# Moving the router's transposes, four low parts and two layout copies in a mixed decoder trunk

## The chip, the cores and the metric

The kernel runs on one core of one Trainium2 chip. The metric is the device time of one execution in microseconds. The kernel before takes 1474.78 us, the median of three runs (1474.64 to 1475.36). The engines are TensorE (PE: matrix products, with PEld for its weight loads), VectorE (DVE), ScalarE (ACT), GpSimd (POOL) and SyncE (SP), which hands the weight transfers to the DMA queue.

## The reference

Two decoder layers over 256 tokens of width 1024. Layer 0 mixes tokens with gated linear attention and channels with a dense SwiGLU; layer 1 mixes with softmax attention (called fox here) and channels with a mixture of 8 experts, of which each token takes 2. The part that matters is the expert layer and the norm ahead of it:

```python
h = rms_norm(x, norm_gain[i, 1]) * (1.0 + sc2) + sh2
logits = (h @ w_router).astype(jnp.float32) + b_router.astype(jnp.float32)
top_vals, top_idx = lax.top_k(logits, TOP_K)
top_w = jax.nn.softmax(top_vals, axis=-1)
combine = jnp.sum(jax.nn.one_hot(top_idx, N_EXPERTS, dtype=jnp.float32)
                  * top_w[..., None], axis=-2)
for e in range(N_EXPERTS):
    y = y + combine[..., e:e + 1].astype(h.dtype) * swiglu(h, w_gate[e], w_up[e], w_down[e])
x = x + g2 * y
```

All values are float32. One expert has three matrices of 1024 x 3584 (14.7 MB each), so the eight experts' weights are 352 MB.

## The kernel before, in words

**Staging.** Every weight comes from memory in 1 MB tiles `raw` (ring of 7, in the expert stage 10). In the attention layers and for half of the experts each tile is split into a rounded high part `whi` (ScalarE, line 224) and the rest `wlo` (VectorE or GpSimd, line 226), and a product is then three passes: high by high, high by low, low by high. The helper `split` may make a tile in several parts, may give some low parts to GpSimd, and may put its high and low parts behind named instructions.

**The router stage**, in the order of the data:

- The attention's output projection `foxo` (lines 247 to 249) ends in eight blocks of 128 columns. `Norm.update` adds each to the residual `xT` (VectorE, line 352), squares it (ScalarE, `n_sq_moe` for block 0 and `n_t_moe` for the others, lines 361 and 364; three `n_t` buffers), adds the squares of blocks 1 to 5 into `n_sq_moe` (GpSimd, line 366), and makes the scaled pair `hr_moe_h` (ScalarE, line 378) and `hr_moe_l` (VectorE, line 379). TensorE sums `n_sq_moe` and the squares of blocks 6 and 7 over the channels into `n_ss_moe` (line 372).
- `narrow` multiplies the pair by the router's weights into `rlogT` (8 blocks, two products each, lines 493 and 494), copies it to `rlog_t` (VectorE), and turns it to tokens in rows, `rlog`, with four small products (lines 503 to 506).
- `Norm.col` makes the root `n_moe_r` (GpSimd, line 423) from `n_ss_moe`.
- `residual` transposes `xT` into four banks `xr` of PSUM, 16 transposes of 128x128 (TensorE, line 992). `tokens` makes the token pair `m_h` (ScalarE, line 1030) and `m_l` (VectorE, line 1032) from it, and `residual_out` copies it to `xres`.
- `positions` makes the logits `rlg`, compares them in pairs (`req`, `rgt`), sums and thresholds to the mask `msk` (VectorE, lines 1012 to 1017), and counts places with three small products `pos`. The one-hot `oh` follows.
- `gather` (line 1137) multiplies the token pair by the one-hot: 32 passes for the first expert, which give its input `g`. The counts `cnt` (line 1047) feed `ranks`, VectorE's chain of small steps (`rkc`, `rku`, `rkm`, `rkt`) that ends in `order`, the experts sorted by load. SyncE reads `order` (line 1271) to know which expert's weights come after those of expert 0's first stage, which are already loaded.
- The expert loop then alternates a large slot (split weights) with a small one (raw weights, two column halves, line 1256).

`hows` gives the first four weight tiles of the expert stage their treatment; the second has all four low parts on GpSimd, the third two of four.

**What sets the order.** A scheduler puts the instructions of each engine into a fixed order by their dependences, by a simulated time and by priority: what is wrapped in `urgent` comes first. `after(i, ...)` adds an order against the instruction `i`, without a wait, to those instructions of the block that run on the engine of `i`; to instructions of other engines it adds nothing. Within an engine the order is then kept on the chip, and a first instruction that waits holds all behind it. `first` is a dictionary of such instructions: `r` is the root on GpSimd, `msk` the mask on VectorE, `hi` the last token copy on ScalarE, `lo` the one-hot on VectorE, `g` the last low part of `g` on VectorE.

The layout copies `g2s` (line 1111, called `gs` in the trace, since both are slices of one tile) put the expert gate's two halves one above the other for the small slots.

## Time and profile before

| | |
|---|---|
| median of three runs | 1474.78 us |
| the profiled execution's own time | 1478.52 us |
| its span | 1476.8 us |
| TensorE busy | 1419.3 us (96%) |
| VectorE busy | 961.7 us (65%) |
| ScalarE busy | 695.1 us (47%) |
| GpSimd busy | 80.5 us (5%) |
| bytes moved by the weight queue | 486.87 MB |

The span runs from the first to the last instruction of the profiled execution, whose own time is 3.7 us above the median. Starts in the trace are microseconds from the start of the span. A busy share is an average over stages; the router stage, near 570 to 606 us, is short, and its order is read from the timeline and from the chain of waits. A product appears in two passes where its operands are full float32, so that a count in the trace can be twice that of the program. In a timeline the last brackets give the idle time before an instruction and what ended it.

### The profile page before, as it was taken

How to read it: one execution, taken by the hardware profiler on the slowest of the kernel's cores; microseconds unless marked ns; L12 is line 12 of the kernel's file. 1: busy time of each engine (PE TensorE's matmuls, PEld its weight loads, DVE VectorE, ACT ScalarE, POOL GpSimd, SP SyncE). 2: the span in 40 equal slices, each digit the busy share in tenths (PEclk: the TensorE clock that was granted, in tenths of full speed). 3: DMA queues.
4: the chain of work that ended last, by engine and by line, in shares of the span. 5: the costliest groups of instructions: out<-in, count | busy, mean ns of one | idle time of the engine just before them, and what ended most of it. 6: DMA issues, size and time to landing. Idle time of an engine off the chain costs nothing.

```text
span 1476.8 us, 21633 instructions
## 1 busy us (share of the span) xinstructions
PE 1419.3 (96%) x8443; PEld 1073.4 (73%) x8443; DVE 961.7 (65%) x1292; ACT 695.1 (47%) x982; POOL 80.5 (5%) x87
## 2 busy tenths in 40 slices
PE   6999999999999998999999999999999999999996
PEld 2899999999999997864756664656475556475453
DVE  7786897778977786662744764556574456574353
ACT  3653644344565565552644463445264346254241
POOL 2000200000132124000000000000000000000000
PEclk9999999999999999899999999999999999999998
DMA  9996578898865432699999999999999999999994
GB/s 318 362 340 226 189 269 313 296 345 279 286 178 161 127 103 86 252 403 395 409 402 402 409 409 409 409 402 402 409 409 409 409 401 404 409 409 408 410 398 189
DMA packets 183000, 488.86 MB, mean 331 GB/s; under 512 B 10815, under 2 KB 51913, under 8 KB 182890
## 3 DMA queue, kind: packets, MB, share of 16 engines
q1 hardware_dynamic: 182602, 486.87, 87.7%
q8 instruction: 68, 1.11, 0.3%
q10 hardware_dynamic: 288, 0.52, 0.1%
q14 instruction: 42, 0.34, 0.1%
HBM read 486.32 MB, written 1.05 MB: 330 GB/s over the span
## 4 chain that ended last, share of the span: by engine, by line
PE 81%; DMA 9%; DVE 7%; issue 1%; SPq 1%; ACT 0%; DVEq 0%; ACTq 0%
PE mo L1256 8%; PE mo L243 6%; PE mo L241 6%; PE mo L242 6%; PE md L1256 6%; DMA raw<-in_moe_w_up_dram 4%; PE gu L247 3%; DVE wlo L226 3%; PE gu L249 3%; PE gu L248 3%; PE md L243 3%; DMA raw<-in_moe_w_down_dram 3%; PE md L242 3%; PE md L241 3%; PE dn L247 2%; PE dn L248 2%
## 5 line engine op out<-in xcount | busy, mean ns | idle before, releaser
L226 DVE TENSOR_TENSOR wlo<-raw,whi 128x1024 fp32r<-128x1024 f32 (+2 forms) x481 | 569.0, 1232 | 92.2 <-ACT whi L224 90.9
L224 ACT CAST whi<-raw 128x1024 fp32r<-128x1024 f32 (+2 forms) x491 | 487.5, 1051 | 262.4 <-PE gu L248 67.3
L1256 PE MATMUL mo<-raw,gs 128*64 128x512 f32 (+1 forms) x1024 | 203.7, 543 | 9.9 <-DMA raw<-in_moe_w_up_dram 8.4
L241 PE MATMUL mo<-whi,g 128*128 128x512 f32 x448 | 175.9, 393 | 0.0
L242 PE MATMUL mo<-whi,g 128*128 128x512 f32 x448 | 175.5, 392 | 0.0
L1256 PEld LDWEIGHTS mo<-raw,gs 128*64 128x64 f32 x1024 | 70.3, 137 | 131.1 <-issue 95.5
L243 PE MATMUL mo<-wlo,g 128*128 128x512 f32 x448 | 153.0, 399 | 1.0 <-DVE wlo L226 0.5
L1352 DVE TENSOR_TENSOR msg<-msg,mo 128x512 f32<-128x512 f32 (+1 forms) x16 | 9.9, 620 | 171.6 <-PE mo L1256 171.6
L243 PEld LDWEIGHTS mo<-wlo,g 128*128 128x128 f32 x448 | 83.2, 189 | 35.9 <-issue 13.8
L1256 PE MATMUL md<-raw,gs 128*64 128x512 f32 x448 | 108.8, 603 | 0.0
L241 PEld LDWEIGHTS mo<-whi,g 128*128 128x128 f32 x448 | 84.6, 189 | 19.2 <-issue 1.6
L242 PEld LDWEIGHTS mo<-whi,g 128*128 128x128 f32 x448 | 84.7, 189 | 18.1
L322 DVE SCALAR_TENSOR_TENSOR adacc<-raw,csil,adacc 128x1024 f32<-128x1024 f32 x70 | 90.0, 1286 | 10.3 <-DMA raw<-in_ada_w_dram 9.9
L249 PE MATMUL gu<-h_ffn_h,wlo 128*128 128x256 f32 x320 | 90.5, 284 | 0.0
L248 PE MATMUL gu<-h_ffn_l,whi 128*128 128x256 f32 x320 | 90.1, 282 | 0.0
L247 PE MATMUL gu<-h_ffn_h,whi 128*128 128x256 f32 x320 | 89.9, 283 | 0.0
L241 PE MATMUL md<-whi,act_h 128*128 128x512 f32 x192 | 76.7, 400 | 0.5 <-ACT whi L224 0.5
L242 PE MATMUL md<-whi,act_l 128*128 128x512 f32 x192 | 76.1, 397 | 0.0
L1350 ACT ACTIVATE msg<-mo 128x512 f32<-128x512 f32 (+1 forms) x16 | 8.7, 544 | 132.6 <-PE mo L1256 132.6
L1175 ACT CAST act_h<-actT 128x512 fp32r<-128x512 f32 x24 | 13.3, 589 | 116.2 <-PE actT L1240 116.2
L1256 PEld LDWEIGHTS md<-raw,gs 128*64 128x64 f32 x448 | 28.2, 136 | 51.5 <-issue 51.2
L243 PE MATMUL md<-wlo,act_h 128*128 128x512 f32 x192 | 62.2, 398 | 1.4 <-DVE wlo L226 1.3
(488 smaller groups left out, 2706.1 us busy)
## 6 DMA issues: line engine op xcount, KB each, us to landing
raw<-in_moe_w_gate_dram SPq DMA_DIRECT2D x112, 1024.0 KB, 17.1
raw<-in_moe_w_up_dram SPq DMA_DIRECT2D x112, 1024.0 KB, 16.3
raw<-in_moe_w_down_dram SPq DMA_DIRECT2D x112, 1024.0 KB, 16.9
raw<-in_ada_w_dram SPq DMA_DIRECT2D x48, 1024.0 KB, 7.1
raw<-in_fox_w_in_dram SPq DMA_DIRECT2D x16, 1024.0 KB, 5.9
raw<-in_ffn_w_gate_dram SPq DMA_DIRECT2D x14, 1024.0 KB, 5.3
raw<-in_ffn_w_up_dram SPq DMA_DIRECT2D x14, 1024.0 KB, 6.5
raw<-in_ffn_w_down_dram SPq DMA_DIRECT2D x14, 1024.0 KB, 5.3
```

The lines of the kernel that those rows point to most:

```text
L224: nc.scalar.copy(hi[:, s], raw[:, s])
L226: (nc.gpsimd if i in pool else nc.vector).tensor_tensor(lo[:, s], raw[:, s], hi[:, s].bitcast(F32), op=ALU.subtract)
L241: nc.tensor.matmul(ps, ah, wh, start=first, stop=False)
L242: nc.tensor.matmul(ps, al, wh, start=False, stop=False)
L243: return nc.tensor.matmul(ps, ah, wl, start=False, stop=last)
L247: i = nc.tensor.matmul(ps, wh, ah, start=first, stop=False)
L248: nc.tensor.matmul(ps, wh, al, start=False, stop=False)
L249: nc.tensor.matmul(ps, wl, ah, start=False, stop=last)
L322: nc.vector.scalar_tensor_tensor(a, raw[:, kk, :], csil[:, k:k + 1], a, op0=ALU.mult, op1=ALU.add)
L1175: acts["i"] = nc.scalar.copy(ah, v)
L1256: nc.tensor.matmul(ps[64 * i:64 * (i + 1), 0:n], a, w[:, i * n:(i + 1) * n], start=first, stop=last)
L1352: nc.vector.tensor_mul(sg, sg, ps[:, 0:hw])
```

## The change

Three edits. The 16 transposes of `residual` get an order behind the last router product. The second weight tile's low parts, which are GpSimd's, were named to come behind the root `first["r"]`, and are now named to come behind the mask `first["msk"]`. The two layout copies are traced after the first gather, with an order behind its last low part.

```diff
-        nc.tensor.matmul(ps[0:n, 0:c], w[:, 0:n], xl, start=False, stop=last)
+        return nc.tensor.matmul(ps[0:n, 0:c], w[:, 0:n], xl, start=False, stop=last)
+
+    narrow_last = {}
...
-            mm_side(ps, w[:, k], n, at(norm.raw, A_, k), k == 0, k == KD - 1)
+            narrow_last["i"] = mm_side(ps, w[:, k], n, at(norm.raw, A_, k), k == 0, k == KD - 1)
...
-        xps = residual()
+        with after(narrow_last["i"]):
+            xps = residual()
...
-        for i in range(2):
-            nc.vector.tensor_copy(g2s[64 * i:64 * (i + 1), :], g2[64 * i:64 * (i + 1), 512 * i:512 * (i + 1)])
...
         urgent(gather)(0, 0, oh0)
+        with after(first["g"]):
+            for i in range(2):
+                nc.vector.tensor_copy(g2s[64 * i:64 * (i + 1), :], g2[64 * i:64 * (i + 1), 512 * i:512 * (i + 1)])
...
-        hows = [(4,), (4, range(4), (), (first["r"],)), (4, range(2), (first["hi"],), (first["lo"],)),
+        hows = [(4,), (4, range(4), (), (first["msk"],)), (4, range(2), (first["hi"],), (first["lo"],)),
```

GpSimd from the end of the projection to the root, before (`wlo` 128x1024 belongs to the projection, 128x512 to the experts):

```order
L226 TENSOR_TENSOR wlo<-raw,whi 128x1024 x4
L366 TENSOR_TENSOR n_sq_moe<-n_sq_moe,n_t_moe_6408 128x256
L366 TENSOR_TENSOR n_sq_moe<-n_sq_moe,n_t_moe_6441 128x256
L366 TENSOR_TENSOR n_sq_moe<-n_sq_moe,n_t_moe_6444 128x256
L366 TENSOR_TENSOR n_sq_moe<-n_sq_moe,n_t_moe_6485 128x256
L366 TENSOR_TENSOR n_sq_moe<-n_sq_moe,n_t_moe_6488 128x256
L423 TENSOR_TENSOR n_moe_r<-n_moe_v,nhalf 128x2
L226 TENSOR_TENSOR wlo<-raw,whi 128x512 x6
```

The same place on GpSimd in the changed kernel:

```order
L226 TENSOR_TENSOR wlo<-raw,whi 128x1024 x4
L366 TENSOR_TENSOR n_sq_moe<-n_sq_moe,n_t_moe_6408 128x256
L226 TENSOR_TENSOR wlo<-raw,whi 128x512 x4
L366 TENSOR_TENSOR n_sq_moe<-n_sq_moe,n_t_moe_6441 128x256
L366 TENSOR_TENSOR n_sq_moe<-n_sq_moe,n_t_moe_6444 128x256
L366 TENSOR_TENSOR n_sq_moe<-n_sq_moe,n_t_moe_6485 128x256
L366 TENSOR_TENSOR n_sq_moe<-n_sq_moe,n_t_moe_6488 128x256
L423 TENSOR_TENSOR n_moe_r<-n_moe_v,nhalf 128x2
L226 TENSOR_TENSOR wlo<-raw,whi 128x512 x2
```

Four of the six low parts have moved from behind the root to between the first and the second addition. On ScalarE the squares of blocks 5, 6 and 7, which stood among the last scaled copies, now stand behind all of them.

TensorE from the last transposes to the small products, before (the transposes of banks 0 and 2 stand further ahead, among the projection's last products):

```order
L503 MATMUL rlog<-ident,br_c 128x8
L992 MATMUL xr_6587<-ident,xT 128x128 x2
L992 MATMUL xr_6589<-ident,xT 128x128 x4
L372 MATMUL n_ss_moe_6523<-ones,n_t_moe_6521 128x1
L372 MATMUL n_ss_moe_6524<-ones,n_t_moe_6521 128x1
L493 MATMUL rlogT<-hr_moe_h,wr 16x258
L372 MATMUL n_ss_moe_6523<-ones,n_t_moe_6529 128x1
L372 MATMUL n_ss_moe_6524<-ones,n_t_moe_6529 128x1
L494 MATMUL rlogT<-hr_moe_l,wr 8x258
```

The end of the router products on TensorE in the changed kernel:

```order
L493 MATMUL rlogT<-hr_moe_h,wr 16x258
L494 MATMUL rlogT<-hr_moe_l,wr 8x258
L994 MATMUL xr_6586<-ident,xT 128x128 x4
L994 MATMUL xr_6587<-ident,xT 128x128 x4
L994 MATMUL xr_6588<-ident,xT 128x128 x4
L994 MATMUL xr_6589<-ident,xT 128x128 x4
L505 MATMUL rlog<-ident,br_c 128x8
L506 MATMUL rlog<-two_141,rlog_t 128x8
L508 MATMUL rlog<-two_141,rlog_t 128x8 x2
```

All sixteen transposes stand behind the last `rlogT` product and ahead of all of `rlog`. The first norm sum, from `n_sq_moe`, stands directly behind the projection's last product in the changed kernel, ahead of all `rlogT` products.

VectorE at the start of the ranking, before (`rkc` is the first copy of the counts, `g` the last low part of the first gather):

```order
L1159 TENSOR_TENSOR g<-gs,g 128x256
L1048 COPY rkc<-cnt 128x8
L1049 COPY rku<-rkc 128x8
L1183 CAST ohT_6918<-oht_6915 128x256
L1050 MEMSET rku 128x1
L1159 TENSOR_TENSOR g<-gf_3_6694,g 128x256
L1052 TENSOR_TENSOR rkm<-rku 128x64
```

And in the changed kernel:

```order
L1160 TENSOR_TENSOR g<-gs,g 128x256
L1187 CAST ohT_6918<-oht_6915 128x256
L1050 COPY rkc<-cnt 128x8
L1051 COPY rku<-rkc 128x8
L1160 TENSOR_TENSOR g<-gf_3_6692,g 128x256
L1167 COPY gs<-g_145 64x512 x2
L1052 MEMSET rku 128x1
L1054 TENSOR_TENSOR rkm<-rku 128x64
```

The two layout copies now stand between the copies of the counts and the ranking's comparisons. On TensorE both transposes `oht` now stand ahead of the counts `cnt`; before, one of the two stood behind them. Three small steps of the weights (`comb`, `rsm` twice) have moved ahead of the first one-hot on VectorE.

## Rows read from the trace of the kernel before

**Rows 1.** The page: clock and traffic in 40 slices of 36.9 us.

```profile
PEclk9999999999999999899999999999999999999998
...
GB/s 318 362 340 226 189 269 313 296 345 279 286 178 161 127 103 86 252 403 395 409 402 402 409 409 409 409 402 402 409 409 409 409 401 404 409 409 408 410 398 189
```

**Rows 2.** Busy time by stretch: length, engines with counts, granted clock, transfer share, GB/s.

```profile
600.00:640.00 40.00, 40.00 (x184) 27.45 (x184) 25.53 (x49) 21.40 (x30) 0.00 (x0) 0.94 0.90 352
640.00:700.00 60.00, 60.00 (x256) 34.94 (x256) 25.20 (x24) 24.20 (x28) 0.00 (x0) 1.00 1.01 401
...
1300.00:1400.00 100.00, 96.46 (x430) 58.02 (x428) 49.91 (x47) 41.35 (x47) 0.00 (x0) 1.00 1.02 409
```

**Rows 3.** Waits of SyncE, 580 to 620 us: total, times, longest.

```profile
SPq L1271 <- DVE rku L1079: 21.4, 1, 21.4
```

**Rows 4.** SyncE's transfers in order of time: start, duration, count.

```profile
603.32 2.27 SPq L203 DMA_DIRECT2D raw<-in_moe_w_gate_dram  x4
```

**Rows 5.** Chain of waits around the router: start, length, engine, tile, line, count.

```profile
576.97 0.55 PE xr L992 x5
577.52 0.34 PE n_ss_moe L372 x4
...
578.59 0.12 PE rlogT L493
...
582.50 0.46 PE rlog L506 x4
...
583.65 0.71 DVE req L1012
584.36 1.27 DVE rgt L1013
...
588.53 0.81 DVE msk L1017
...
591.64 7.06 PE ga L1137 x32
...
598.94 0.65 PE cnt L1047 x4
599.59 0.31 PE oht L1181
...
600.71 0.43 PE mo L242
```

**Rows 6.** Busy time by stretch around the router.

```profile
580.00:584.00 4.00, 2.44 (x22) 2.02 (x20) 2.27 (x9) 1.00 (x2) 2.26 (x2) 1.00 0.37 97
584.00:585.00 1.00, 0.00 (x0) 0.00 (x0) 1.00 (x2) 1.00 (x3) 1.00 (x2) 0.61 1.02 422
592.00:600.00 8.00, 7.96 (x39) 7.69 (x38) 5.60 (x19) 4.31 (x10) 0.00 (x0) 0.50 0.01 2
604.00:605.00 1.00, 1.00 (x5) 0.79 (x4) 0.83 (x6) 0.05 (x1) 0.00 (x0) 0.65 0.73 102
```

**Rows 7.** GpSimd in order of time: start, duration, line, operation, count, idle before.

```profile
570.50 0.74 POOL L366 TENSOR_TENSOR n_sq_moe<-n_sq_moe,n_t_moe 128x256 f32<-128x256 f32 x1 [7.22 <-ACT n_t_moe L364]
573.38 3.31 POOL L366 TENSOR_TENSOR n_sq_moe<-n_sq_moe,n_t_moe 128x256 f32<-128x256 f32 x4 [2.15 <-ACT n_t_moe L364]
...
582.95 7.58 POOL L226 TENSOR_TENSOR wlo<-raw,whi 128x512 fp32r<-128x512 f32 x6
```

**Rows 8.** ScalarE in order of time, the high parts beside the norm.

```profile
570.74 2.18 ACT L224 CAST whi<-raw 128x512 fp32r<-128x512 f32 x4
```

**Rows 9.** VectorE in order of time, beside the norm and in the ranking.

```profile
574.60 2.78 DVE L379 SCALAR_TENSOR_TENSOR hr_moe_l<-xT,mod,hr_moe_h 128x256 fp32r<-128x256 f32 x4
577.30 0.86 DVE L352 SCALAR_TENSOR_TENSOR xT<-foxo,mod,xT 128x256 f32<-128x256 f32 x2
...
582.00 0.84 DVE L1111 COPY gs<-g 64x512 f32<-64x512 f32 x2
...
600.62 0.22 DVE L1052 TENSOR_TENSOR rkm<-rku 128x64 f32<-128x64 f32 x1
```

## The prediction

> **What bounds the kernel now.** I read the page's busy slices first, then the granted clock, the transfer queue, the chain of waits and last the single engines around the router. In the slices [rows 1] the traffic falls to 103 and 86 GB/s in slices 15 and 16, is 252 in the next, and then stays near 405 to the end: the experts' weights stream without a break. Over the eight stretches from 640 to 1400 us the transfer engines are full, share 1.01 to 1.03 [rows 2], so a later start of that stream is a later end, one for one. The stream starts when SyncE, which hands out the transfers, has read the list of ranked experts: it waits 21.4 us for VectorE [rows 3] and resumes at 603.32 us [rows 4]. What counts is therefore the chain up to that list [rows 5]: TensorE's norm sums (`n_ss_moe`, 577.52) and router products (`rlogT`, `rlog`, done at 582.96), VectorE's mask (583.65 to 589.34), the gathers (591.64, 7.06 us), the counts (598.94), the ranking. That is one long serial stretch, and everything the change touches lies in it or beside it.
>
> Two costs in it stand out. The gathers run with the clock at 1.2 GHz: it was full from 580 to 584, fell within 584 to 585 and was 0.50 from 592 to 600, though the gathers left TensorE no pause there [rows 6]. And VectorE's small comparisons take 1.27 us instead of about 0.3: each ends as one of GpSimd's low parts ends. GpSimd runs six of them back to back from 582.95, 7.58 us, so 1.26 each [rows 7].
>
> **GpSimd's low parts.** The edit names the mask, a VectorE instruction, as the one to queue behind. An order is kept only between instructions of one engine, and the order of the changed kernel shows that this queues nothing on GpSimd: the old edge, to GpSimd's own root `n_moe_r`, is gone, no new one came, and four parts now stand between the first and the second of the five additions into `n_sq_moe`. Their data are ready: ScalarE makes the high parts from 570.74, the first by 571.3 [rows 8], and GpSimd is free since 571.24 [rows 7]. So four parts take 571.3 to 576.35 (4 x 1.26). Three additions at 0.83 (3.31 / 4) follow, to 578.85. The last one needs its square, which ScalarE now makes behind all scaled copies. Those need the last `xT` updates of VectorE, which start at 577.30 behind four `hr_moe_l` that took 2.78 us beside GpSimd's additions [rows 9]; with GpSimd busy without a break each waits for one GpSimd instruction, and I put the updates at 578.1. Two copies and the square bring it to about 579.95, the addition to 580.7, and TensorE's first norm sum to 580.85 instead of 577.52: +3.3. (Were the square not late it would be 579.8; with the parts a tenth slower beside VectorE's work, as the additions are, 0.83 against 0.74 alone [rows 7], 581.4.) TensorE is in order, so all router products wait behind this sum, though most of their inputs are ready. Before, the same wait was not there: five transposes ran up to it.
>
> What it gives: the mask chain loses four of the six low parts that held it. From the first comparison to the mask's end it now takes 5.69 us (583.65 to 589.34). Alone, four comparisons near 0.27 (a 128x64 one takes 0.22, [rows 9]), a reduction and a threshold come to 1.55. The two parts left on GpSimd wait for high parts that ScalarE makes behind the token copies, as before, and so they fall at about the time of the comparisons: each can cost up to 1.26. Ends 1.55 and 4.1; I take 2.6, one part met in full. Gain 3.1.
>
> The Trainium skill (SBUF — State Buffer, section "Who interferes with whom") says that a VectorE instruction with two SBUF inputs contends with a GpSimd instruction that reads SBUF, and that the later one blocks for the whole of the other. By that alone the comparisons would lose four waits of 1.26 and the edit would give up to 5 us, against the 3.1 taken here; the rows [rows 5, 7] agree on the blocking, but the same rule charges the four `hr_moe_l` that the parts now run beside.
>
> **The transposes.** Sixteen of them. Before, ten stood among the projection's last products and six where TensorE waited for inputs, so they cost little. Ten leave the projection, and it ends at 576.4 instead of 576.97; that gains nothing, for the sum is not there until 580.85. All sixteen now stand between `rlogT` and `rlog`, on the path. At full clock the stretch is: 12 passes of norm sums at 0.085 (4 in 0.34), 16 products at 0.12, 16 transposes at 0.11 (5 in 0.55), 8 small `rlog` passes at 0.115 (4 in 0.46) [rows 5]: 1.02 + 1.92 + 1.76 + 0.92 = 5.62, ending at 586.5, against 582.96: +3.55. That GpSimd's reciprocal root is ready earlier than `rlog` helps nobody but the token copies.
>
> **The clock in that stretch.** TensorE now stands still from 576.4 to 580.85, 4.4 us. Before, it ran dry at 582.96 and the clock was down within 584 to 585 [rows 5, 6], at most 2 us later. So I expect it down when the norm sums begin, or soon after. Did it come back within the stretch? The gathers, of the transposes' shape, ran 7 us without raising it; the experts' dense products did, but only within 604 to 605, after some 4 us (the first still take 0.43 at 600.71) [rows 5, 6]. I take it low to the end. At that level a 512-column product takes 0.43 [rows 5], so a 258-column one 0.215; a transpose what a gather pass takes, 7.06 / 32 = 0.22; a small pass what the counts take, 0.65 / 4 = 0.163. Sum: 16 x 0.215 + 16 x 0.22 + 20 x 0.163 = 3.44 + 3.53 + 3.26 = 10.2, so `rlog` ends at 591.1, +8.15.
>
> **The two layout copies.** They leave VectorE's queue at 582.00 (0.84 us, [rows 9]), where `rlog` was not yet done: gain about 0. They now stand, with the cast `ohT`, in front of the ranking's first step on VectorE, and the counts stand behind both `oht` transposes: 0.84 of copies, of which some lies in waiting. I take +0.9 with the 0.31 of the transpose that the counts now stand behind [rows 5] (bounds 0 if all of it hides, 1.5 if none). Three small instructions of the weights have also moved ahead of the first one-hot: two behind the mask, covered by the token parts, one in front: +0.25.
>
> **Sum.** Mask: `rlog` at 591.1, comparisons 0.7 later as before, 2.6 of chain: 594.4 against 589.34, +5.1. One-hot +0.25, ranking +0.9: the stream of weights starts about 6.2 us later. Gathers low in both. The profiled execution took 1478.52 with a span of 1476.8, 3.7 above the median of the three runs, 1474.78; I add the shift to the median unchanged: 1474.78 + 6.2 = 1481.0.
>
> **Rivals.**
> - *The clock comes back during the stretch* (or falls late into it). For it: `rlogT` is dense once the sums are through. Against: the 7 us of gathers. Transposes and `rlog` at full level save 1.77 + 0.38: +4.05, 1478.8.
> - *The clock does not fall at all.* The stall is there, with full-level products: `rlog` 586.5, mask 589.8, then 0.25 and 0.9: +1.65, 1476.4; a mask chain at its upper end 1477.9. Against it: the fall after 582.96.
> - *Not slower: the gathers run at full clock.* The transposes put dense work closer to the mask, and the chain behind is shorter, 3.3 us instead of 6.4, so TensorE may enter the gathers at full level, at 0.115 instead of 0.22 a pass: 32 x 0.105 = 3.4 less, 0.1 less in the counts. It decides if the clock survives both the standstill before the sums and the one before the one-hot; on top of +1.65 it gives -1.8, 1473.0, and with both low parts missing the comparisons 1471.9. Against it: two waits, each longer than what sufficed before.
> - *The end doesn't follow the routing*, because the stream has slack that the trace hides. For it: from 600 to 640 the share is 0.90, not full. Against: share 1.01 to 1.03 from 640 on [rows 2]. About +0.7, 1475.5.
>
> **How the numbers follow.** Forecast 0.48, clock back 0.20, clock kept 0.16, gathers at full clock 0.09, no coupling 0.07. A measurement of this kernel tells about 0.2% from no change, 2.95 us, so slower is above 1477.7 and faster below 1471.8. Slower: 0.46 of the forecast, 0.16 of the second and 0.05 of the third, 0.67. Faster: half of the fourth, which with a clean mask chain stands at that bound, 0.05. The rest, 0.28, is no change. The range of 8 in 10 runs from the no-coupling case to the forecast with parts that meet the mask chain at its upper end (+1.5) and half a microsecond more in the norm: 1475.5 to 1483.0; left out are the fourth case, half of the fifth and a small tail above.
>
> **What would show it.** Right: four low parts on GpSimd between 571 and 576.5; the first norm sum near 580.9 with TensorE idle for over 4 us before it; the granted clock at half there; sixteen transposes at 0.2 each ahead of `rlog`; comparisons near 0.3 but for one or two; SyncE resuming near 609.5. Wrong: a norm sum before 579 (the parts started later or ended sooner), transposes at 0.11 (clock kept), a stream that resumes late but ends on time (slack), or gathers at 0.11.

## The result, and the profile after

The changed kernel takes 1484.62 us (median of 4 runs, 1484.45 to 1485.94), the kernel before in the same comparison 1475.07 us (4 runs, 1474.64 to 1475.80). The medians are 9.55 us apart, a ratio of 1.0065; the ratio on record is 1.0057 with a 95% interval of 1.0037 to 1.0077. So the changed kernel is slower by some 9.5 us, where 6.2 us was forecast, with 1481.0 and a range up to 1483.0. The direction is as forecast, the size is not, and the time lies outside the range.

The profiled execution of the changed kernel took 1484.45 us with a span of 1482.7 us. Between the two profiled executions the span grew by only 5.9 us (1482.7 - 1476.8). So the first thing to see is that the profiles do not hold the whole 9.5 us. Read them for what the edit did first. GpSimd of the changed kernel in order of time (start, duration, line, operation, count, idle before):

```profile
571.09 0.74 POOL L366 TENSOR_TENSOR n_sq_moe<-n_sq_moe,n_t_moe 128x256 f32<-128x256 f32 x1 [7.23 <-ACT n_t_moe L364]
572.03 5.41 POOL L226 TENSOR_TENSOR wlo<-raw,whi 128x512 fp32r<-128x512 f32 x4 [0.20 <-ACT whi L224]
577.40 2.63 POOL L366 TENSOR_TENSOR n_sq_moe<-n_sq_moe,n_t_moe 128x256 f32<-128x256 f32 x3
581.23 0.72 POOL L366 TENSOR_TENSOR n_sq_moe<-n_sq_moe,n_t_moe 128x256 f32<-128x256 f32 x1 [1.20 <-ACT n_t_moe L364]
...
591.51 2.53 POOL L226 TENSOR_TENSOR wlo<-raw,whi 128x512 fp32r<-128x512 f32 x2 [5.00 <-ACT whi L224]
```

This answers [rows 7]. The four low parts stand between the first and the second addition, as forecast, and only two parts are left for the time of the comparisons. The first addition starts 0.59 us later than before (571.09 against 570.50), which comes from ahead of the change; below, all times are counted from that addition. VectorE beside it and in the ranking, in the same columns:

```profile
574.96 4.48 DVE L379 SCALAR_TENSOR_TENSOR hr_moe_l<-xT,mod,hr_moe_h 128x256 fp32r<-128x256 f32 x4
579.37 0.86 DVE L352 SCALAR_TENSOR_TENSOR xT<-foxo,mod,xT 128x256 f32<-128x256 f32 x2
...
594.20 0.27 DVE L1016 TENSOR_TENSOR req<-req,tie 128x128 f32<-128x128 f32 x1
...
606.46 0.85 DVE L1167 COPY gs<-g 64x512 f32<-64x512 f32 x2
...
607.47 0.23 DVE L1054 TENSOR_TENSOR rkm<-rku 128x64 f32<-128x64 f32 x1
```

Against [rows 9]: four `hr_moe_l` took 4.48 us instead of 2.78 beside the low parts, and the last two `xT` updates started at 579.37 instead of 577.30. A comparison that meets no low part (594.20) takes 0.27 us. The two copies stand right ahead of the ranking's first step. The chain of waits (start, length, engine, tile, line, count), with lines that answer to [rows 5]:

```profile
582.00 1.02 PE n_ss_moe L372 x4
...
587.45 2.47 PE xr L994 x16
...
590.46 0.46 PE rlog L508 x4
...
591.61 1.32 DVE req L1014
592.93 1.27 DVE rgt L1015
...
595.15 0.17 DVE msk L1019
...
597.65 7.06 PE ga L1138 x32
...
606.16 0.76 PE mo L241
```

and the stretches of the same kernel that answer to [rows 6] (length, engines with counts, granted clock, transfer share, GB/s):

```profile
576.00:582.00 6.00, 0.99 (x9) 0.78 (x7) 5.12 (x8) 1.88 (x6) 4.59 (x6) 1.00 0.00 0
582.00:588.00 6.00, 6.00 (x32) 5.15 (x33) 0.64 (x3) 0.00 (x0) 0.71 (x1) 0.50 0.21 46
589.00:592.00 3.00, 1.90 (x17) 1.64 (x15) 0.92 (x4) 3.00 (x7) 0.49 (x1) 1.00 0.29 120
593.00:609.00 16.00, 12.45 (x51) 11.74 (x52) 12.99 (x40) 5.93 (x14) 1.04 (x1) 0.50 0.00 1
```

TensorE has 0.99 us of work from 576 to 582. From 582 to 588 the norm sums and router products run at 1.2 GHz. The clock comes back within the sixteen transposes, which take 2.47 us instead of the 3.53 that I worked out for the low level, and it is low again for the gathers, which take 7.06 us as before. SyncE's transfers in order of time, and a later stretch of the kernel:

```profile
610.16 2.31 SPq L203 DMA_DIRECT2D raw<-in_moe_w_gate_dram  x4
```

```profile
640.00:700.00 60.00, 60.00 (x254) 34.50 (x252) 30.81 (x30) 25.63 (x30) 0.00 (x0) 1.00 1.02 402
```

The stream restarts at 610.16 us instead of 603.32 [rows 3, 4], and from 640 to 700 us it is as full as before [rows 2]. From the first addition to the restart the kernel before needs 32.82 us (570.50 to 603.32) and the changed one 39.07 us: +6.25, where the prediction had +6.2. At SyncE's last write of the output the difference is 5.35 us, still counted from that addition (1469.01 for the start of the two last writes before, 1474.95 after, less 0.59): 0.9 us is given back behind the restart.

It is given back at once. ScalarE's first split of the next weights and the third group of transfers behind the restart, before and then in the changed kernel:

```profile
604.95 2.18 ACT L224 CAST whi<-raw 128x512 fp32r<-128x512 f32 x4 [4.96 <-PE mo L242]
...
617.71 11.47 SPq L203 DMA_DIRECT2D raw<-in_moe_w_down_dram  x3
```

```profile
610.41 2.19 ACT L224 CAST whi<-raw 128x512 fp32r<-128x512 f32 x4 [4.42 <-PE mo L242]
...
623.17 11.47 SPq L203 DMA_DIRECT2D raw<-in_moe_w_down_dram  x3
```

Counted from the first addition, both are 4.87 us later, not 6.25. ScalarE's split waits for TensorE's expert products. The first of these starts 5.62 us later (606.16 against 599.95, less 0.59), but the clock comes back 3.1 us behind it instead of 4.8 (granted 0.86 from 609 to 610 us here, 0.65 from 604 to 605 before [rows 6]), so that the twelfth, at which ScalarE is let go, is 4.88 later. In all fourteen profiles the third group starts 12.8 to 13.3 us behind that split, whatever the restart did. So the third group follows the expert products and no longer the moment at which SyncE reads the ranking.

So the forecast of the mechanism held in the profiles up to the restart, and some 4 us of the measured 9.5 were not in them. Executions of one and the same kernel come in groups some 4 us apart, which the mean granted clock of an execution tells apart.

| mean granted clock | runs | time, us |
|---|---|---|
| before, 0.987 to 0.990 | 48 | 1472.64 to 1477.02, median 1474.61 |
| before, 0.985 to 0.986 | 48 | 1477.57 to 1479.84, median 1479.16 |
| before, 0.980 to 0.981 | 5 | 1483.52 to 1484.20 |
| changed, 0.986 to 0.987 | 3 | 1479.80 to 1481.88 |
| changed, 0.983 to 0.984 | 9 | 1483.10 to 1485.94, median 1484.41 |

(The 101 runs of before are those of the three later comparisons; of the changed kernel the first and e5.) By their times the four runs of before in the first comparison belong to the first row; by time and clock all four of the changed kernel belong to the last; and the profile of before that the prediction was read from (1478.52 us, clock 0.986) belongs to the second row. Below, the first and the second row of before are called its short and its long form.

### The profile page after: what moved, and what is told of

Same layout as the page of the kernel before. It is cut to its first block, busy times and chain, and to the rows that moved or that the text cites. A ratio compares the mean times of both kernels' runs of the same rounds, so it can differ in the third digit from the quotient of the medians.

```text
span 1482.7 us, 21629 instructions
## 1 busy us (share of the span) xinstructions
PE 1422.3 (96%) x8443; PEld 1075.6 (73%) x8443; DVE 962.4 (65%) x1292; ACT 694.4 (47%) x982; POOL 80.2 (5%) x87
## 4 chain that ended last, share of the span: by engine, by line
PE 81%; DVE 8%; DMA 8%; issue 1%; SPq 1%; ACT 1%; POOL 0%; DVEq 0%; ACTq 0%; POOLq 0%
PE mo L1260 8%; PE mo L243 6%; PE mo L241 6%; PE md L1260 6%; PE mo L242 6%; DVE wlo L226 4%; DMA raw<-in_moe_w_up_dram 4%; PE gu L247 3%; PE gu L249 3%; PE gu L248 3%; PE md L243 3%; DMA raw<-in_moe_w_down_dram 3%; PE md L241 3%; PE md L242 3%; PE dn L247 2%; PE dn L248 2%
## 5 line engine op out<-in xcount | busy, mean ns | idle before, releaser
L1179 ACT CAST act_h<-actT 128x512 fp32r<-128x512 f32 x24 | 13.3, 589 | 115.3 <-PE actT L1244 115.3
```

The costliest lines, as they stand in the source:

```text
L1179: acts["i"] = nc.scalar.copy(ah, v)
```

## The experiments

The expectations of e1 to e4 stand under a first pair of theories: (A) in the quicker executions the gathers run at full clock, so that the router stretch itself is shorter there; (B) the difference between executions of one kernel lies outside that stretch, 570 to 606 us. e1 decided it for B. The expectations of e5 to e12 stand under the pair that followed: (A) the change costs the forecast some 6 us at the router, and the rest of the 9.5 is the distance between two forms of execution, decided long before the router; (B) the change costs 9.5 us in every form. The starts that decide between them are collected in one table, each a difference of two starts in the timelines of one kernel: from the first addition into `n_sq_moe` on GpSimd to the first norm sum, from there to the first gather, to the first expert product, and to the restart of the weight stream on SyncE (its first `raw<-in_moe_w_gate_dram`). The last two columns go on behind the restart: the start of the third group of transfers (the first `raw<-in_moe_w_down_dram`) and of the last write, each from the first addition, as a difference to before. The table counts the first norm sum of before from the timeline, where it starts at 577.36; [rows 5] has 577.52, because the chain counts its overlap with the transposes ahead of it to these.

```profile
577.36 0.51 PE L372 MATMUL n_ss_moe<-ones,n_sq_moe 128*128 128x1 f32 x4
```

| kernel | first addition at | to norm sum | to gather | to product | to restart | sum | third group | last write |
|---|---|---|---|---|---|---|---|---|
| before | 570.50 | 6.86 | 14.28 | 8.31 | 3.37 | 32.82 | 0 | 0 |
| changed | 571.09 | 10.91 | 15.65 | 8.51 | 4.00 | 39.07 | +4.87 | +5.35 |
| e1 before again | 566.20 | 6.85 | 14.30 | 8.30 | 3.37 | 32.82 | -0.14 | -0.10 |
| e2 edits 1 and 3 | 564.84 | 6.23 | 14.55 | 8.51 | 4.00 | 33.29 | +0.19 | -0.15 |
| e3 edit 2 | 570.47 | 10.53 | 13.64 | 8.52 | 3.14 | 35.83 | +3.48 | +4.41 |
| e4 low parts behind the mask | 570.92 | 6.85 | 11.10 | 10.18 | 3.44 | 31.57 | -0.79 | -0.41 |
| e5 changed again | 570.54 | 10.92 | 15.64 | 8.51 | 4.00 | 39.07 | +4.97 | +5.75 |
| e6 before, line 309 wide | 567.98 | 6.85 | 14.29 | 8.29 | 3.37 | 32.80 | -0.01 | +0.18 |
| e7 changed, line 309 wide | 566.27 | 10.92 | 15.67 | 8.51 | 4.00 | 39.10 | +4.92 | +5.75 |
| e8 edits 1 and 3, wide | 566.56 | 6.23 | 14.54 | 8.51 | 4.00 | 33.28 | -0.31 | -1.03 |
| e9 edit 2, wide | 570.81 | 10.54 | 13.68 | 8.51 | 3.13 | 35.86 | +3.42 | +4.33 |
| e10 edit 1, wide | 567.58 | 6.23 | 15.01 | 8.51 | 3.13 | 32.88 | -0.02 | +0.59 |
| e11 edit 3, wide | 567.75 | 6.85 | 14.98 | 8.30 | 4.26 | 34.39 | +0.22 | +0.29 |
| e12 as e8, low parts behind the mask | 565.08 | 6.24 | 11.75 | 10.50 | 4.21 | 32.70 | -0.34 | -0.37 |

Edit 1 is the transposes, edit 2 the low parts, edit 3 the copies. The first column moves with the form of the execution, by up to 6 us. The sum depends on the kernel alone: where a kernel ran in two forms (line 309 apart), it agrees within 0.03 us. The last column repeats less well, to 0.9 us for one and the same set of edits (e2, e8). That table separates the two things which the first comparison had mixed.

**e1: the kernel before, once more, unedited.**

> The kernel before, unchanged. Its profiled execution took 1478.5 us, its timed ones 1474.6 to 1475.8. Theory A (the routing stretch has two forms): in the quicker executions TensorE's clock is full in the gathers, which then take about 3.6 us instead of 7.1, so a profile near 1475 shows gathers of 3.6 us and a granted clock above 0.988; one near 1478.5 shows 7.1 us. Theory B (the 3.4 us of the profiled execution lie elsewhere, in the start or in the stream of weights): the gathers take 7.1 us in every profile, and what differs is the time outside 570 to 606 us.

Measured: 1474.38 us (12 runs, 1473.22 to 1479.08), ratio 0.9986 (0.9972 to 1.0001). The profiled execution took 1474.14 us, so a short form was caught. GpSimd and TensorE of it in order of time, first addition, first norm sum and first gather:

```profile
566.20 0.73 POOL L366 TENSOR_TENSOR n_sq_moe<-n_sq_moe,n_t_moe 128x256 f32<-128x256 f32 x1 [7.22 <-ACT n_t_moe L364]
```

```profile
573.05 0.51 PE L372 MATMUL n_ss_moe<-ones,n_sq_moe 128*128 128x1 f32 x4
...
587.35 0.66 PE L1137 MATMUL ga<-oh,m_h 128*128 128x128 f32 x2 [0.82 <-DVE oh L1121]
```

and one stretch far ahead of the router, of before, of the changed kernel and of this one:

```profile
138.00:144.00 6.00, 6.00 (x30) 6.00 (x30) 1.68 (x5) 0.20 (x1) 0.70 (x1) 0.51 0.04 16
```

```profile
138.00:144.00 6.00, 6.00 (x31) 6.00 (x31) 1.84 (x6) 0.59 (x4) 0.69 (x1) 0.52 0.17 64
```

```profile
138.00:144.00 6.00, 6.00 (x53) 6.00 (x53) 3.40 (x5) 2.38 (x2) 0.00 (x0) 1.00 0.00 0
```

All of the 4.3 us lies before the first addition (566.20 against 570.50). From there on the two executions agree to 0.02 us, with gathers of the same length, so A, gathers at full clock, fell, and B held. In the long form the clock is 0.51 and 0.52 from 138 to 144 us, in the short one 1.00, and TensorE is busy throughout in all three: the same stream of products, at half the clock for about 6 us. Ahead of that stretch each has two groups of one-column products of line 309 (`adat`), which start at 134.3 and 136.7 us in before and at 133.3 and 135.7 in e1.

So 1.0 us of the 4.3 is there before the fall; at the third group (208.05 against 203.75) all 4.3 are, and nearly all of the other 3 us arises in the fall. The first microsecond goes with an earlier stretch, in which the clock of before is 0.92 (its line stands under e9). In e1 it is full:

```profile
40.00:50.00 10.00, 10.00 (x84) 9.85 (x84) 8.06 (x18) 6.00 (x12) 0.57 (x2) 1.00 1.09 357
```

The seven profiles with line 309 as it was part in the same way: where the clock is 0.87 to 0.92 from 40 to 50 us (before, changed, e3, e4, e5) it falls again at 138, and where it is 1.00 there (e1, e2) it does not. So the form shows by 50 us, and the fall at 138 us follows in the late executions only.

**e2: without edit 2.**

```
-        hows = [(4,), (4, range(4), (), (first["msk"],)), ...
+        hows = [(4,), (4, range(4), (), (first["r"],)), ...
```

> The changed kernel with GpSimd's low parts back behind the root; transposes and layout copies stay moved. Theory 1 (the standstill before the first norm sum and the low clock behind it cost most): the norm sum starts near 577.5 again, the products and transposes run at full clock (0.12 and 0.11 each), rlog ends near 584.3, the mask again takes about 5.7 us beside six low parts: about 2.4 us over the kernel before in the routing stretch, some 7 less than the changed kernel. Rival (the sixteen transposes on the path cost most): it stays within 3 us of the changed kernel.

Measured: 1474.47 us (12 runs, 1472.68 to 1479.79), ratio 0.9991 (0.9975 to 1.0007). In the table edits 1 and 3 together cost 0.47 us at the restart, less than the 2.4 that was expected, and nothing at the last write: the norm sum 0.63 earlier, the product 0.47 later behind it, the restart 0.63 later behind the product. It takes edit 2 to make the kernel slower (e3).

**e3: edit 2 alone**, the same line the other way round in the kernel before.

```
-        hows = [(4,), (4, range(4), (), (first["r"],)), ...
+        hows = [(4,), (4, range(4), (), (first["msk"],)), ...
```

> The kernel before with only the edit of the low parts; transposes stand ahead of the norm sum, in its wait. Theory 1: the norm sum starts near 581.5, the clock is low behind it, rlog ends near 588.5, about 2 us sooner than in the changed kernel, the stream of weights starts about 3 us sooner (transposes 1.9, copies 0.9): 1481.5. Rival (transposes cost most): it is within 2 us of the kernel before.

Measured: 1478.96 us (12 runs, 1477.18 to 1485.39), ratio 1.0022 (1.0007 to 1.0036). TensorE in order of time:

```profile
579.28 1.16 PE L992 MATMUL xr<-ident,xT 128*128 128x128 f32 x6 [1.80 <-DVE xT L352]
581.00 0.98 PE L372 MATMUL n_ss_moe<-ones,n_sq_moe 128*128 128x1 f32 x4 [0.56 <-POOL n_sq_moe L366]
...
594.64 0.66 PE L1137 MATMUL ga<-oh,m_h 128*128 128x128 f32 x2 [0.82 <-DVE oh L1121]
```

The norm sum is late by 3.67 us, as in the changed kernel less 0.38, but six transposes are done in the wait ahead of it and none stand behind it. The stretch is 35.83 us, +3.0. So at the restart edit 2 alone costs 3.0 and edits 1 and 3 alone 0.5, but together 6.25: 2.8 us more. By the table 1.7 of these arise between norm sum and gather, where edit 1 puts sixteen transposes behind products that edit 2 has made late, and 1.0 ahead of the norm sum, where the 0.63 that edits 1 and 3 gain is lost in the wait for GpSimd and 0.38 more goes. Where the products are not late, the same transposes cost next to nothing (e10). Edits 1 and 2 without edit 3 were not run, so that the 1.7 is edit 1's alone is argued and not shown. At the last write the shares are others: edit 2 alone is 4.4 us late (the medians of e3 and e1 are 4.6 apart), edits 1 and 3 are 0.15 to 1.03 early, and the three together 5.35 to 5.75 late, 1.1 to 2.5 more than the parts.

**e4: the low parts really behind the mask.** A small addition on GpSimd reads the mask, and the six low parts are ordered behind it, so that they wait on GpSimd itself.

```
+            first["mk"] = nc.gpsimd.tensor_tensor(mk, msk[:, 0, :], msk[:, 1, :], op=ALU.add)
...
-(4, range(4), (), (first["r"],)), (4, range(2), (first["hi"],), (first["lo"],))
+(4, range(4), (), (first["mk"],)), (4, range(2), (first["hi"],), (first["lo"], first["mk"]))
```

> The kernel before with one small GpSimd addition that reads the mask, and GpSimd's six low parts ordered behind that addition, so that they really come behind the mask. Theory 1: the comparisons take about 0.3 us each, the mask's chain 1.6 us instead of 5.7; the first one-hot then meets a low part, up to 1.2 us: the stream of weights starts 2.5 to 4 us sooner, 1471 to 1472.5. With TensorE's pause 4 us shorter the gathers may also see another clock: if they run full, 3.4 us less again. Rival (the end doesn't follow the routing): no change.

Measured: 1476.68 us (12 runs, 1471.39 to 1478.49), ratio 0.9995 (0.9982 to 1.0009). The gathers start 3.2 us earlier (11.10 against 14.28 behind the norm sum), since no comparison meets a low part, but the first expert product is 1.9 later behind them: 1.25 us remains at the restart, less than the 2.5 to 4 expected, and 0.4 at the last write; the times show no gain. What the edit's words say would be worth a microsecond at the restart; the edit as it stands does something else.

**e5: the changed kernel, once more, unedited.**

> The changed kernel once more, unedited, with more runs. Theory A (executions come in two forms some 4.3 us apart, parted by the granted clock of TensorE at 137 to 144 us, long before the router; the first comparison set four executions of before in the short form against four of the changed kernel in the long one): the runs fall into two groups, near 1480 and near 1484.5, and the median ratio to before is about 1.004 (1.003 to 1.005), +6 us; a profile in the short form starts the first norm sum near 577.7 us, one in the long form near 582. Theory B (the changed kernel is 9.5 us slower in every form): all runs stand at 1483 or above and the ratio stays at 1.006 or more.

Measured: 1483.58 us (8 runs, 1479.80 to 1484.41) against 1478.81 us (31 runs), ratio 1.0039 (1.0023 to 1.0055). Three of the eight runs are at 1479.8 to 1481.9 with a clock of 0.986 or 0.987, the rest at 1483.1 to 1484.4 with 0.984: two groups, as A had it, and the difference of 9.5 us did not come again. The profile is of the long form and has the stretch of 39.07 us.

**e6: the kernel before with line 309 widened.** The edit is meant to take away what the clock fell on; e7 to e12 carry it too.

```
-                nc.tensor.matmul(ps[:, k:k + 1], a[:, k * P:(k + 1) * P], ones[:, 0:1], ...)
-            ada_out(i, j, ps[:, 0:KD])
+                nc.tensor.matmul(ps[:, 64 * k:64 * k + 64], a[:, k * P:(k + 1) * P], ones[:, 0:64], ...)
+            ada_out(i, j, ps[:, 0:64 * KD:64])
```

> The kernel before, with the 144 small products of the modulation (line 309) written with 64 equal columns instead of one; the sum reads one column of each, so what is computed is the same. Theory A: in the long form the granted clock falls from 1.00 to 0.50 at 137.5 us, behind two rows of 16 such products, and stays there until 143.5; in the short form the same products stand there and it does not fall. If these products are what the clock falls on, the fall at 137 to 144 us goes, all executions are in the short form, 1472 to 1475.5 us with no group near 1479, and the ratio to before is 0.997 to 0.999. The products themselves: between 0 and 144 x 0.1 us on TensorE, mostly beside weight loads. Rival (the form is decided by something else, earlier, at 30 to 50 us, and the fall at 137 us only follows): two groups as in before, ratio 0.9995 to 1.003. Rival (the wider products cost time of their own): one group, but at 1477 or above.

Measured: 1475.42 us (12 runs, 1474.25 to 1477.76), ratio 0.9984 (0.9974 to 0.9994). Eleven of the twelve runs lie below 1476.3, one at 1477.76, and half of them above the expected 1475.5; of the 101 runs of before 53 lie at 1477.5 or above. The stretch of 138 to 144 us:

```profile
138.00:144.00 6.00, 6.00 (x53) 6.00 (x52) 2.68 (x7) 2.58 (x3) 0.69 (x1) 1.00 0.07 25
```

The fall is gone, and with it nearly all of the long form. The earlier stretch is that of a long form, though, and the profile's first addition, at 567.98, is 1.8 us later than in e1:

```profile
40.00:50.00 10.00, 10.00 (x74) 9.85 (x74) 6.56 (x15) 5.79 (x12) 0.57 (x2) 0.88 1.09 355
```

So both hold in part, the theory and its first rival: the form shows at 30 to 50 us, and with the narrow products of line 309 the clock falls a second time in executions that were late there. With the wide ones it stays at 1.00, though their first two groups start as late as in before (134.46 against 134.34); so it does in e10 and e11, whose clock from 40 to 50 us is 0.92 and 0.91. The edit takes away the some 3 us of the fall and leaves the first microsecond. The clock also falls from 190 to 200 us, to 0.83, but there e1 has the same.

**e7: the changed kernel with line 309 widened.**

> The changed kernel with the same edit of line 309. Theory A: one group, near 1479.5 (1478.5 to 1481), so +5 to +7 us to the kernel with that edit alone and a ratio of 1.002 to 1.004 to before; granted clock 1.00 at 137 to 144 us, first norm sum near 577.5 us, and the router's stretch as in the profile of the changed kernel (TensorE idle for some 5 us, then 0.50 of the clock). Theory B (9.5 us in every form): 1482 or above.

Measured: 1480.37 us (12 runs, 1478.33 to 1484.29), ratio to before 1.0027 (1.0012 to 1.0042). TensorE and SyncE in order of time:

```profile
577.19 1.00 PE L372 MATMUL n_ss_moe<-ones,n_sq_moe 128*128 128x1 f32 x4 [5.01 <-POOL n_sq_moe L366]
```

```profile
605.37 2.32 SPq L203 DMA_DIRECT2D raw<-in_moe_w_gate_dram  x4
```

The norm sum starts at 577.19, as expected of a short form, behind the same wait of 5.01 us as in the changed kernel, and the stretch is 39.10 us. Against e6 the median is 4.95 us longer. With the long form out of the way the change costs 5 us, not 9.5. Four of the runs, at 1481.8 to 1484.3, lie above the expected group.

**e8: edits 1 and 3, line 309 widened.**

> The changed kernel without its edit 2 (GpSimd's low parts wait for the norm's column as in before) and with line 309 as in the two others: a version that may be faster than both kernels. Theory A with edits 1 and 3 worth nothing: as the kernel before with line 309 edited, within 1 us. If the copies behind the gather cost what I forecast: +0.9. If transposes behind the products bring the logits forward by what stood between the products in before (6 transposes, 0.87 us): -0.9. In numbers 1471 to 1475, ratio to before 0.996 to 0.999.

Measured: 1473.77 us (12 runs, 1472.49 to 1476.79), ratio 0.9975 (0.9962 to 0.9988), the fastest kernel here, ahead of both. Most of the gain against before is the form: the first addition stands at 566.56, without a fall at 138 us. How much of the 1.65 us between the medians of e8 and e6 belongs to edits 1 and 3 stays open: they make the stretch 0.5 us longer, as in e2, but at the last write this execution is 1.03 us ahead of before, and e2 only 0.15.

**e9: edit 2 alone, line 309 widened.**

> The kernel before with edit 2 alone and line 309 widened as in e6, so that one form of the executions is left. From the first addition of the norm on GpSimd to the restart of the weight stream on SyncE, before and e6 take 32.8 us, the changed kernel 39.1, edit 2 alone (e3) 35.8. Theory A (edit 2 costs 3.0 alone, edits 1 and 3 alone 0.5, and the remaining 2.7 come only when edit 1's sixteen transposes stand in the stretch in which the clock has fallen): 35.8 +-0.3 here, and a time of e6 + 3 = 1478.4 (1477.3 to 1479.6), ratio 1.000 to 1.002 to before, whose own runs are in two forms. Rival (e3 was a chance of its form; edit 2 costs 5 to 6 alone): 38 or more, 1480 or above.

Measured: 1480.17 us (12 runs, 1477.93 to 1483.13), ratio 1.0018 (1.0004 to 1.0033). The stretch is 35.86 us, as expected, so edit 2 alone costs 3.0 at the restart in both executions profiled, and 4.3 to 4.4 at the last write. The time missed, in part because it was added up from the 3.0: five runs lie at 1477.9 to 1478.9, the expected group, seven at 1480.2 to 1483.1. The profiled execution is of these (1483.13), and its first addition is at 570.81 with no fall at 138 us. Its stretches, and then those of before:

```profile
30.00:40.00 10.00, 8.48 (x34) 3.83 (x32) 7.78 (x21) 3.21 (x8) 2.93 (x3) 0.74 1.09 326
40.00:50.00 10.00, 9.40 (x62) 8.54 (x61) 6.55 (x16) 6.55 (x14) 0.00 (x0) 0.83 1.10 350
138.00:144.00 6.00, 6.00 (x52) 5.95 (x51) 2.55 (x9) 1.04 (x5) 0.69 (x1) 1.00 0.51 172
```

```profile
30.00:40.00 10.00, 7.70 (x35) 3.85 (x34) 9.86 (x25) 4.36 (x9) 2.23 (x3) 0.90 1.11 335
40.00:50.00 10.00, 10.00 (x78) 9.85 (x77) 6.70 (x15) 5.83 (x12) 0.57 (x2) 0.92 1.09 356
```

The clock was lower from 30 to 50 us (0.74 and 0.83 against 0.90 and 0.92), and from 40 to 50 TensorE was not busy throughout. So an execution can be late without the fall behind line 309, from the earlier stretch alone. Why that one goes one way or the other stays open.

**e10: edit 1 alone, line 309 widened.**

> The kernel before with edit 1 alone and line 309 widened. Edits 1 and 3 together gave 33.3 instead of 32.8 us from first addition to restart: norm sum 0.6 earlier, first expert product 0.5 later behind the norm sum, restart 0.6 later behind that product. Theory: the earlier norm sum is edit 1's and the copies' 0.85 us is edit 3's, so edit 1 alone gives 32.2 to 32.8, time 1475 +-1. Rival: sixteen transposes in a row hold the logits up: 33.3 or more.

Measured: 1475.85 us (12 runs, 1474.09 to 1481.22), ratio 0.9993 (0.9977 to 1.0008); stretch 32.88 us, +0.08 to e6, so a little above the expected 32.2 to 32.8. The norm sum gains 0.62 and the transposes give 0.72 back ahead of the gathers.

**e11: edit 3 alone, line 309 widened.**

> The kernel before with edit 3 alone and line 309 widened. Theory: the two copies, 0.85 us together, stand between the ranking's steps and delay the restart by that: 33.3 to 33.7 from first addition to restart, time 1476 +-1. Rival: they are hidden beside TensorE's gathers, which last 7.06 us: 32.8.

Measured: 1475.85 us (12 runs, 1473.04 to 1476.39), ratio 0.9987 (0.9973 to 1.0000); stretch 34.39 us, +1.59 to e6, more than either theory had. Half is as expected: the copies stand in the ranking, and the restart is 0.89 later behind the product. The other half is at the place that they left. VectorE and GpSimd of e6, then of e11:

```profile
579.47 0.84 DVE L1111 COPY gs<-g 64x512 f32<-64x512 f32 x2
...
581.13 0.71 DVE L1012 TENSOR_TENSOR req<-rlg 128x128 f32<-128x128 f32 x1
```

```profile
579.22 1.23 POOL L423 TENSOR_TENSOR n_moe_r<-n_moe_v,nhalf 128x2 f32<-128x2 f32 x1 [5.04 <-PE rlogT L494]
580.42 7.57 POOL L226 TENSOR_TENSOR wlo<-raw,whi 128x512 fp32r<-128x512 f32 x6
```

```profile
580.89 1.40 DVE L1012 TENSOR_TENSOR req<-rlg 128x128 f32<-128x128 f32 x1
```

```profile
578.98 0.71 POOL L423 TENSOR_TENSOR n_moe_r<-n_moe_v,nhalf 128x2 f32<-128x2 f32 x1 [5.05 <-PE rlogT L494]
579.66 7.57 POOL L226 TENSOR_TENSOR wlo<-raw,whi 128x512 fp32r<-128x512 f32 x6
```

With the copies gone GpSimd's root takes 0.71 instead of 1.23 us, its low parts begin 0.53 us earlier behind the first addition (11.91 against 12.44), and the first comparison, which starts no earlier, now lasts 1.40 instead of 0.71. The copies had held the low parts off by half a part. With edit 1 in place the sign of this half turns: from norm sum to gather 14.54 in e8, 15.01 in e10. Nearly all of the 1.59 is gone behind the restart: the third group of transfers is 0.22 us late and the last write 0.29.

**e12: e8 with the low parts behind the mask**, by the edit of e4.

> A version for speed: edits 1 and 3, line 309 widened, and GpSimd's six low parts put behind a small addition on GpSimd that reads the routing mask, as in e4 (so they wait for the mask's data and not for an instruction of another engine in issue order). In e4 this brought the gathers forward by 3.2 us, of which 1.25 were left at the restart (31.6 from first addition to restart). Theory: with edits 1 and 3 the same gain: 31.8 to 32.4, time 1472.5 (1471 to 1473.8), ratio 0.996 to 0.998 to before. Rival: VectorE's low parts of the next weights wait behind the moved ones, and the copies come on top: 33.3 or more, 1473.8 or above.

Measured: 1474.80 us (12 runs, 1472.77 to 1476.03), ratio 0.9984 (0.9970 to 0.9998); stretch 32.70 us, 0.6 less than e8, less than expected. The time is above the expected range too; against e8 no gain shows. GpSimd and VectorE in order of time:

```profile
580.15 8.50 POOL L226 TENSOR_TENSOR wlo<-raw,whi 128x512 fp32r<-128x512 f32 x6
```

```profile
584.17 3.35 DVE L226 TENSOR_TENSOR wlo<-raw,whi 128x512 fp32r<-128x512 f32 x2
587.44 1.37 DVE L1079 TENSOR_SCALAR comb<-comb,rsm 128x8 f32<-128x8 f32 x2
```

The six parts now run to 588.65, beside VectorE's own two low parts (3.35 us, where the changed kernel needs 1.28) and a small step of 1.37 that took 0.36 there, both ahead of the gathers' copies: 2.0 of the 2.8 us gained at the gathers go there.

## Why the prediction was wrong

The step that failed is the last one of the sum: "I add the shift to the median unchanged". The shift itself, read from one profiled execution, was +6.2, and the profiled executions show +6.25 at the restart. But the profile's page gave 1478.52 us for its own execution against a median of 1474.78 for the timed runs, and I wrote that difference down without asking what it was. It was the distance between two forms. The four timed runs of before were in the short one, the four of the changed kernel in the long one. Taken like for like, the long groups stand at 1484.41 and 1479.16 us, 5.25 apart, and e7 and e6 4.95 apart; with the 4.3 us between the forms of before (570.50 against 566.20) that makes the 9.5. Why all eight runs fell as they did is not known: of the changed kernel's 12 runs 9 were in the long form, of before's 101 runs 53 were not in the short one, and 12 runs are too few to tell whether the change favours it. If each run fell by itself with these shares, four short ones against four long ones would come about once in sixty times (an estimate, 48/101 and 9/12 to the fourth power), so the runs of one comparison may not be independent, or the change may favour the long form. No run here decides it.

A second step failed by less: "a later start of that stream is a later end, one for one". Of the 6.25 us at the restart 4.87 are left at the third group of transfers and 5.35 to 5.75 at the last write, because the third group follows TensorE's expert products and not the restart; what adds to it on the way to the last write was not followed. In e11 the restart is 1.6 us late and the end 0.3; in e3 they are 3.0 and 4.4.

Point by point:

- **Low parts.** Right, in place and mechanism. The norm sum moved by 4.05 us (10.91 against 6.86), where I had 3.33 with 3.9 as the upper case. Mis-sized: four low parts took 5.41 instead of 5.04, and VectorE's four `hr_moe_l` 4.48 instead of 2.78, so that the last square was late by more.
- **Clock.** Right that it falls in the wait and that the products run low. Wrong that it stays low to the end of the stretch: the transposes took 2.47 instead of 3.53, and `rlog` is at full level. Logits done at 590.92 against 582.96, +7.4 from the first addition, where I had +8.15. These two errors partly cancelled.
- **Mask.** Two low parts met the first two comparisons, 1.32 and 1.27, and the others took 0.3: one part more than I took. The first comparison began 7.96 later than before and the mask ended 5.98 later, so the chain gave 2.0 back and not 3.1; net of 0.59 the mask is +5.4, where I had +5.1. The 0.25 for the one-hot was 0.03 (mask to gather 2.33 against 2.30).
- **The rule weighed.** The Trainium skill (SBUF — State Buffer, section "Who interferes with whom") has the later instruction wait for the whole of the earlier one. The trace agrees on both sides: comparisons of 1.32 and 1.27 beside low parts of 1.26 each (2.53 for two), 0.27 without. The same rule's charge on the `hr_moe_l` was in the sum with 0.8 us (updates at 578.1 instead of 577.30); it was 1.48 (579.37 less 0.59).
- **Copies and transposes.** From the gather to the restart +0.83 (12.51 against 11.68), as +0.9 had it. At the restart edit 3 alone costs 1.6 and edit 1 alone nothing, which the sum, made for all three together, did not show.
- **Rivals.** "The clock comes back during the stretch" happened in part and was worth less than the 2.2 us that I gave it: from norm sum to logits 8.92 us (582.00 to 590.92) instead of 10.2. "The end doesn't follow the routing" fell, but 0.5 to 0.9 of the 6.25 us was given back behind the restart, which I had at nothing.

## What to carry to other kernels

An order named between instructions of two engines queues nothing in this program: a stage is held back only by an instruction of its own engine that needs the data (e4), and then the work that was held back meets something else. Costs of edits on one serial stretch do not add where one edit changes what the next one runs beside: 3.0 and 0.5 alone, 6.25 together at the restart. Nor is the event that a stretch ends in what the end of the kernel waits for: read the cost again at the last write (4.4, -0.15 and 5.35 for the same kernels). And where a profile's own time and the median of its runs differ by more than the effect in question, count from a common event ahead of the change, and compare executions of one form, before a shift is added to a median.

## What the runs showed of the hardware

One kernel's executions differed by 4.3 us in where they entered the router. One microsecond of it goes with TensorE's granted clock from 40 to 50 us, 0.92 against 1.00; nearly all the rest with a second fall that only the late executions had, 0.51 instead of 1.00 from 138 to 144 us, though the stream of products had no pause there in either. Widening 144 products from one column to 64 took the second fall away, also in executions that were late at 50 us (e6, e10, e11), and brought the median from 1478.81 to 1475.42 us. A stage behind such falls is moved as a whole: the 32.8 us of the router stretch agreed to 0.02 us between executions that entered it 4.3 us apart.

The clock also decides what a delay costs later. In the changed kernel it came back 3.1 us behind the first expert product instead of 4.8, and 0.7 us of the 5.62 by which that product was late was gone by the twelfth.
